# First pair's weight sums on GpSimd, third pair's in the norm's scratch with two accumulating loads; the condition row spread by matmuls, x on one queue

## The chip, the core and the metric

The kernel runs on one core of one Trainium2 chip. The metric is the device time of one execution in microseconds; of a kernel, the median over its runs. In the text, PE is TensorE, DVE is VectorE, ACT is ScalarE, POOL is GpSimd and SP is SyncE, whose queue issues most of the loads. Each engine works through its own instructions in order, so an instruction that waits holds everything that stands behind it on that engine.

## What is computed

A decoder trunk of two layers on a sequence of 512 tokens, model width 1024. Each layer is a half-step SwiGLU feed-forward (FFN), a token mixer (a short gated convolution in layer 0, native sparse attention in layer 1), and a second half-step FFN: six sub-layers, s = 0 to 5, with FFNs at s = 0, 2, 3 and 5. Each sub-layer starts with an RMS norm whose scale and shift, and ends with a gate, that come from a conditioning vector c:

```python
cond = jax.nn.silu(c)
for i in range(DEPTH):
    mod = (cond @ ada_w[i] + ada_b[i]).reshape(bsz, 3, 3, D_MODEL)
    shift, scl, gate = mod[:, :, 0], mod[:, :, 1], mod[:, :, 2]
    h = adaln(x, norm_g[i, 0], shift[:, 0], scl[:, 0])
    x = x + HALF * gate[:, 0, None, :] * swiglu(h, ffn_w_in[i, 0], ffn_w_out[i, 0])
    ...
def swiglu(h, w_in, w_out):
    g, u = jnp.split(h @ w_in, 2, axis=-1)
    return (jax.nn.silu(g) * u) @ w_out
```

All data are float32.

## The kernel before

**Layout.** x lies transposed in SBUF, eight tiles x[0] to x[7] of 128 partitions (128 model columns) by 512 tokens. A float32 product is made of three fast matmuls: each operand is split into a rounded part and the rest (`split`, L168: ACT copies to the rounded type, L169; DVE subtracts, L170), and `mm3` (L172 to L175) adds hi·hi, hi·lo and lo·hi. So each weight tile costs a load (tag `wraw`, three buffers, issued by SP), one ACT pass (`whi`) and one DVE pass (`wlo`).

**The start.** SP loads x[0] to x[5], then the condition c as a load that repeats its row over all 128 partitions (L97, 512 KB), then the first tiles of ada_w (`adaraw`, 512 KB each); GpSimd's queue loads x[6], x[7] and two small tables. `Norm.start` squares the x tiles on ACT (L271), adds them on DVE into `nacc` (L273), sums over partitions on PE (`pr`, L275), and takes the reciprocal root on DVE (`rsqrt`, L201 to L209). ACT applies SiLU to c (L112). DVE multiplies each `adaraw` tile with `cond` and sums (L124): 144 of these give all shifts, scales and gates.

**The FFNs at s = 2, 3 and 5** (function `ffn`, weights f = 1, 2, 3) have 22 hidden tiles. For the first three (j = 0, 1, 2) gate and up are plain products: in `head_start` (matmuls named `hs`) for the first half of the tokens and then for the second half, then `pair`. Each half has its own norm: `Norm.finish` runs a reciprocal root on DVE under high priority and then makes diagonal tiles `dg` (L262) that PE spreads (L263, `pr`); `Norm.piece` (L312 to L315) makes h from them. The later 19 tiles (j = 3 to 21) use `seven_products`: a Strassen-like scheme in which gate and up together take seven half-size products instead of eight. It needs sums of weight quarters. In words, for each j, which the text calls a pair (gate and up):

- `qa`, two quarters wide: SP loads quarters 11 of gate and 22 of up into its halves (L490, L491), and one load on GpSimd's queue adds quarter 21 of gate to both halves (L493, an accumulating load);
- `raw` (L495), the whole gate tile, and `a22`, one quarter of up (L496);
- `qb`, two adds: `qa`'s second half plus raw's first half (L497), and that plus raw's second half (L498), both on DVE;
- then the splits of raw, qa, a22 and qb (ACT `whi`, `qah`, `qbh`; DVE `wlo`, `qal`, `qbl`), the seven products of 12 matmuls each (PE, named `gu`), of which ACT copies the first away at once (`p1`, L520), since its PSUM columns are used again, and the sums of the products on DVE (`e`, L526 to L532).

"First pair" is j = 3, "second" j = 4, "third" j = 5. Where `qa` lies is set by a list (L553 to L555): pool `swa` has two buffers called `own`; the first three pairs use `own`, so the third has to wait until the first pair's `qa` has been split. The pairs behind them turn through two freed pieces of the norm's output (tags `hhi1`, `hlo1`) and `own`. The norm's squares use a scratch of two tiles of 128x512 (`sq`), which is idle from the end of the norm until the next sub-layer's squares.

Hidden tiles are grouped in `FOUR` (6, 6, 6, 4); after each of the first three groups eight output products `y` follow (L567 to L570). The order of the instructions on each engine comes from a scheduler, which places each by priority and by its dependences; the order below is what it made.

Of the kernel before, what the change touches and what calls it, by code (L numbers as in the profile page):

```python
# [13 lines left out]
F32 = mybir.dt.float32  # L14
F32R = mybir.dt.float32r
I32 = mybir.dt.int32
AF = mybir.ActivationFunctionType
ALU = mybir.AluOpType
# [4 lines left out]
P = 128  # L23
D = 1024
T = 512
HT = T // 2
KD = D // P
# [26 lines left out]
def decoder_kernel(ctx, tc, xT, cT, ng, adaw, adab, ffi, ffo, cwi, cw, cwo,  # L54
                   nwi, nwg, pos, w1, w2, qg, kg, nwo, rb, onehot, rowok, out):
    nc = tc.nc

    def pool(es, name, bufs, **kw):
        kw.setdefault("reuse_waits", "tile")
        return es.enter_context(tc.tile_pool(name=name, bufs=bufs, **kw))  # L60
# [7 lines left out]
    wp = pool(ctx, "wp", 4)  # L68
# [8 lines left out]
    def psum(name, tag="mm"):  # L77
        tag = next(six) if tag == "mm" else {"pr": "o"}.get(tag, tag)
        return ps.tile([P, T], F32, name=name, tag=tag, bufs=2)
# [4 lines left out]
    def tmp(name, n=T, tag="t"):  # L84
        bufs, size = TAGS[tag]
        return tp.tile([P, n], F32, name=name, tag=tag, padded_shape=[P, size], bufs=bufs)
# [3 lines left out]
    ap = ada_es.enter_context(tc.tile_pool(name="ada", bufs=4))  # L90
    cond = ap.tile([P, D], F32, name="cond", bufs=1)
    x = [cst.tile([P, T], F32, name=f"x{d}") for d in range(KD)]
    ngs = cst.tile([P, NSUB * KD], F32, name="ngs")
    adabs = cst.tile([P, NSUB * NMOD], F32, name="adabs")
    for d in range(KD):
        (nc.sync if d < KD - 2 else nc.gpsimd).dma_start(x[d], xT[d])
    nc.sync.dma_start(cond, bass.AP(tensor=cT.tensor, offset=cT.offset, ap=[[0, P], [1, D]]))  # L97
    nc.gpsimd.dma_start(ngs, ng)
    nc.gpsimd.dma_start(adabs, adab)
    rowm = cst.tile([P, 1], F32, name="rowm")  # L100
# [4 lines left out]
    ones = cst.tile([P, P], F32, name="ones")  # L105
# [3 lines left out]
    kgs = cst.tile([P, 3], F32, name="kgs")  # L109
    mods = cst.tile([P, NSUB * NMOD], F32, name="mods")  # L110

    nc.scalar.activation(cond, cond, AF.Silu)  # L112

    def mod(s, kind, d):
        c = s * NMOD + kind * KD + d
# [52 lines left out]
    def split(src, hi, lo):  # L168
        nc.scalar.activation(hi, src, AF.Copy)  # L169
        nc.vector.tensor_tensor(lo, src, hi, ALU.subtract)  # L170

    def mm3(o, sh, sl, mh, ml, first, last):  # L172
        nc.tensor.matmul(o, sh, mh, start=first, stop=False)  # L173
        nc.tensor.matmul(o, sh, ml, start=False, stop=False)  # L174
        nc.tensor.matmul(o, sl, mh, start=False, stop=last)  # L175
# [219 lines left out]
    class Hidden:  # L395
# [4 lines left out]
        def keep(self, af):  # L400
            hi = self.fa.tile([P, T], F32R, name="ahi", tag="a")
            lo = self.fa.tile([P, T], F32R, name="alo", tag="a")
            split(af, hi, lo)
            self.hi.append(hi)
            self.lo.append(lo)
# [63 lines left out]
    def ffn(s, f, nrm, nxt, w0, ahead):  # L469
        with ExitStack() as es:  # L470
# [3 lines left out]
            nj = 2  # L474
# [3 lines left out]
            def seven_products(j):  # L478
                QT = KD * P // 2
                quart = lambda c, k: ffi[f, j, c].rearrange("p k n -> p (k n)")[:, k * QT:(k + 1) * QT]  # L480
                raw = wp.tile([P, 2, QT], F32, name="wraw", tag="wraw", bufs=3)
                whi = wp.tile([P, 2, QT], F32R, name="whi", tag="whi", bufs=3)
                wlo = wp.tile([P, 2, QT], F32R, name="wlo", tag="wlo", bufs=3)
                qa = next(sums)()
                a22 = tmp("a22")
                qb = swa.tile([P, 2, QT], F32, name="qb")
                ah_, al_ = (sw.tile([P, 2, QT], F32R, name=f"qa{e}", bufs=2) for e in "hl")
                bh_, bl_ = (sw.tile([P, 3, QT], F32R, name=f"qb{e}") for e in "hl")
                e = sw.tile([P, 4, HT], F32, name="e")
                nc.sync.dma_start(qa[:, 0], quart(0, 0))  # L490
                nc.sync.dma_start(qa[:, 1], quart(1, 1))  # L491
                a21 = quart(1, 0)
                nc.gpsimd.dma_start(qa, bass.AP(tensor=a21.tensor, offset=a21.offset, ap=[a21.ap[0], [0, 2], a21.ap[1]]),  # L493
                                    accum_op=ALU.add)
                nc.sync.dma_start(raw.rearrange("p a b -> p (a b)"), ffi[f, j, 0].rearrange("p k n -> p (k n)"))  # L495
                nc.sync.dma_start(a22, quart(1, 1))  # L496
                nc.vector.tensor_tensor(qb[:, 0], qa[:, 1], raw[:, 0], ALU.add)  # L497
                nc.vector.tensor_tensor(qb[:, 1], qb[:, 0], raw[:, 1], ALU.add)  # L498
                split(raw, whi, wlo)
                split(qa, ah_, al_)  # L500
                split(a22, bh_[:, 0], bl_[:, 0])
                split(qb, bh_[:, 1:3], bl_[:, 1:3])

                def product(o, w, b):
                    for i in range(KD // 2):
                        c = slice(i * P, (i + 1) * P)
                        mh, ml = b(i)
                        mm3(o, w[0][:, c], w[1][:, c], mh, ml, i == 0, i == KD // 2 - 1)

                a11, a12 = [(whi[:, i], wlo[:, i]) for i in range(2)]  # L510
                s3, s1 = [(ah_[:, i], al_[:, i]) for i in range(2)]
                a22, s2, s4 = [(bh_[:, i], bl_[:, i]) for i in range(3)]
                t1, t2, t3, t4 = nrm.blocks
                lo, hi = slice(0, HT), slice(HT, T)
                ox, oy, oz = psum("gu"), psum("gu"), psum("gu")
                both = lambda o: o.rearrange("p (a b) -> p a b", a=2)
                product(oy[:, lo], a11, nrm.quarter(0, 0))
                p1 = tmp("p1", HT, "xr")
                with tc.high_priority():
                    nc.scalar.activation(p1, oy[:, lo], AF.Copy)  # L520
                product(ox[:, lo], a12, nrm.quarter(1, 0))
                product(oy[:, hi], s3, t3)
                product(oy[:, lo], s1, t1)
                product(oz[:, hi], a22, t4)
                product(ox[:, hi], s2, t2)
                nc.vector.tensor_tensor(e[:, 0:2], both(ox), p1[:, None].to_broadcast([P, 2, HT]), ALU.add)  # L526
                nc.vector.tensor_tensor(e[:, 2], oy[:, hi], e[:, 1], ALU.add)
                nc.vector.tensor_tensor(e[:, 1:4:2], oy[:, None, lo].to_broadcast([P, 2, HT]), e[:, 1:3], ALU.add)
                product(oz[:, lo], s4, nrm.quarter(1, 1))
                nc.vector.tensor_tensor(e[:, 1:3], both(oz), e[:, 1:3], ALU.add)  # L530
                nc.scalar.activation(e[:, 0:2], e[:, 0:2], AF.Silu)
                nc.vector.scalar_tensor_tensor(e[:, 0:2], e[:, 0:2], -1.0, e[:, 2:4], op0=ALU.mult, op1=ALU.mult)  # L532
                keep(e[:, 0:2].rearrange("p a b -> p (a b)"))
# [4 lines left out]
            with ExitStack() as tf_es:  # L538
                nrm.alloc_seven(hp, pool(tf_es, "tf", 1))
                h = nrm.hi, nrm.lo  # L540
                with ExitStack() as hw_es:
# [8 lines left out]
            nj += 1  # L550
            sw_es = es.enter_context(ExitStack())

            own, quarter = (partial(swa.tile, [P, 2, KD * P // 2], F32, name="qa", bufs=2),  # L553
                            [partial(hp.tile, [P, 2, KD * P // 2], F32, name="qa", tag=t) for t in ("hhi1", "hlo1")])
            sums = chain((own, own, own), cycle((*quarter, own, own)))  # L555
            sw = pool(sw_es, "sw", 1)
            shift(sw, 64)
            for j in range(nj):
# [1 line left out]
            for p, (j0, j1) in enumerate(FOUR):  # L560
                for j in range(max(j0, nj), j1):
                    seven_products(j)
                n = j1 - j0
                a = (hid.hi[j0:j1], hid.lo[j0:j1])
                if p < len(FOUR) - 1:
                    for d in range(KD):
                        w = ffn_out(f, d, 1, j0, j1)  # L567
                        o = psum("y")
                        project(o, w, 0, a, [(k, k) for k in range(n)], True, True)
                        nc.vector.scalar_tensor_tensor(x[d], o, mod(s, 2, d), x[d], op0=ALU.mult, op1=ALU.add)  # L570
# [4 lines left out]
            for i, d in enumerate(range(0, KD, 2)):  # L575
                if i < 2:
                    ws.append(ffn_out(f, d, 2, j0, j1))
                else:
                    t = (2, 0)[i - 2]
                    to = [tt.tile([P, KD // 2, HT], F32R, name=f"t{e}{t}").rearrange("p a b -> p (a b)") for e in "hl"]  # L580
                    raw = swa.tile([P, 2, KD * P // 2], F32, name="qa", bufs=2).rearrange("p a b -> p (a b)")
# [18 lines left out]
            for d, t in [(d, 0) for d in range(6, KD)] + [(d, HT) for d in range(KD)]:  # L600
                o = psum("ty")
# [631 lines left out]
    ada_es.close()  # L1233
    nrm, nxt = nxt, Norm(3)
    w = ffn(2, 1, nrm, nxt, w, ffn_ahead(2))
    nrm, nxt = nxt, Norm(4)
    w = ffn(3, 2, nrm, nxt, w, lambda: nsa_in(4))
    nrm, nxt = nxt, Norm(5)
    w = nsa(4, nrm, nxt, w, ffn_ahead(3))
    ffn(5, 3, nxt, None, w, None)  # L1240


# [73 lines left out]
```

## Time and profile before

| | us |
|---|---|
| three runs | 1999.37, 2007.13, 2008.69 |
| median | 2007.13 |
| the profiled execution | 2008.19 |
| its span, first to last instruction | 2006.4 |
| PE busy in it | 1932.2 (96%) |
| DVE, ACT, POOL busy | 1493.1, 874.8, 203.1 |

The profile is of one execution. Busy PE is the time in which matmuls were in flight; PE at half its clock is as busy as at full clock, so the granted clock has to be read beside it. "Idle before" an instruction is the time its engine stood still ahead of it, with the instruction or load that ended the wait. "DMA share" is the mean busy share of the 16 DMA engines. Times in the text are counted from the start of the span. The stages in it: FFN s = 0 to 367, convolution to about 570, the FFNs from about 575, 920 and 1640, attention from about 1280.

### The profile page before, as it was taken

The numbers are of one execution on the slowest core, as the hardware profiler recorded it, in microseconds if no ns is written. First come the engines' busy times: TensorE is split into PE (matmuls) and PEld (weight loads), VectorE is DVE, ScalarE is ACT, GpSimd is POOL, SyncE is SP. The second block draws the span as 40 slices with busy tenths as digits, with TensorE's granted clock in tenths as the row PEclk, the third lists the DMA queues.
The fourth block names the chain that finished last, engine by engine and source line by source line (L and its number), as shares of the span: only waits on it lengthen the run. The fifth ranks groups of instructions, "written<-read, shape, count | busy, mean of one in ns | idle before, by whom it ended". The sixth has DMA issues, their size and how long they took to land.

```text
span 2006.4 us, 32443 instructions
## 1 busy us (share of the span) xinstructions
PE 1932.2 (96%) x12644; PEld 1747.7 (87%) x12644; DVE 1493.1 (74%) x2597; ACT 874.8 (44%) x1410; POOL 203.1 (10%) x279
## 2 busy tenths in 40 slices
PE   5999999999988999999999999999999899999999
PEld 3878888798888898999989899999888689898989
DVE  7878888674457686868868686886787978786866
ACT  3322222232225353434535343455777866343532
POOL 0000000100010000000000000001434430000000
PEclk9999999999998999999999999999999999999999
DMA  8888988432235664634566453243211223665622
GB/s 308 304 315 311 328 316 325 156 105 84 84 105 146 165 167 126 163 101 116 157 169 169 131 160 102 68 137 107 54 48 28 84 63 100 181 175 154 170 69 74
DMA packets 113047, 307.40 MB, mean 153 GB/s; under 512 B 13883, under 2 KB 14155, under 8 KB 112892
## 3 DMA queue, kind: packets, MB, share of 16 engines
q1 hardware_dynamic: 97164, 274.81, 40.4%
q0 software_dynamic: 15728, 30.51, 8.9%
q8 instruction: 99, 1.62, 0.3%
q14 instruction: 56, 0.46, 0.1%
HBM read 302.12 MB, written 3.15 MB: 152 GB/s over the span
## 4 chain that ended last, share of the span: by engine, by line
PE 69%; DVE 14%; DMA 9%; ACT 4%; issue 3%; SPq 1%; POOL 0%; DVEq 0%; ACTq 0%; POOLq 0%
PE gu L173 10%; PE gu L174 10%; PE gu L175 10%; DMA adaraw<-in_adaw 7%; PE y L173 6%; PE y L175 6%; PE y L174 6%; DVE wlo L170 3%; DVE adaraw L124 3%; PE cv L174 2%; PE cv L173 2%; PE cv L175 2%; PE hs L173 1%; PE hs L174 1%; PE hs L175 1%
## 5 line engine op out<-in xcount | busy, mean ns | idle before, releaser
L169 ACT ACTIVATE whi<-wraw 128x1024 fp32r<-128x1024 f32 (+2 forms) x283 | 281.8, 999 | 499.8 <-PE y L174 264.5
L170 DVE TENSOR_TENSOR wlo<-wraw,whi 128x1024 fp32r<-128x1024 f32 (+2 forms) x283 | 326.4, 1155 | 59.9 <-ACT whi L169 57.8
L174 PE MATMUL gu<-hlo,whi 128*128 128x256 f32 (+1 forms) x808 | 258.5, 320 | 0.0
L173 PE MATMUL gu<-hhi,whi 128*128 128x256 f32 (+1 forms) x808 | 258.2, 320 | 0.0
L175 PE MATMUL gu<-hhi,wlo 128*128 128x256 f32 (+1 forms) x808 | 257.6, 319 | 0.0
L173 PE MATMUL y<-ahi,whi 128*128 128x512 f32 x587 | 230.2, 395 | 2.9 <-ACT ahi L169 2.9
L174 PE MATMUL y<-alo,whi 128*128 128x512 f32 x587 | 228.7, 392 | 0.8 <-DVE alo L170 0.8
L175 PE MATMUL y<-ahi,wlo 128*128 128x512 f32 x587 | 229.0, 393 | 0.0
L124 DVE CUSTOM_DVE_ANT_0 adaraw<-adaraw,cond 128x1024 f32<-128x1024 f32 x144 | 174.8, 1223 | 37.1 <-DMA adaraw<-in_adaw 34.8
L173 PEld LDWEIGHTS gu<-hhi,whi 128*128 128x128 f32 x808 | 151.7, 188 | 13.0
L175 PEld LDWEIGHTS gu<-hhi,wlo 128*128 128x128 f32 x808 | 151.6, 188 | 12.3
L174 PEld LDWEIGHTS gu<-hlo,whi 128*128 128x128 f32 x808 | 151.7, 188 | 12.0
L493 POOL DMA_DIRECT2D qa<-in_ffi x57 | 68.6, 1204 | 816.8 <-DVE wlo L170 228.4
L173 PE MATMUL gu<-th,qah 128*128 128x256 f32 x456 | 128.9, 283 | 9.6 <-ACT p L520 9.6
L173 PEld LDWEIGHTS y<-ahi,whi 128*128 128x128 f32 x587 | 109.8, 188 | 30.6 <-ACT ahi L169 7.4
L174 PEld LDWEIGHTS y<-alo,whi 128*128 128x128 f32 x587 | 110.6, 188 | 26.9 <-DVE alo L170 3.2
L175 PEld LDWEIGHTS y<-ahi,wlo 128*128 128x128 f32 x587 | 110.6, 188 | 23.8
L570 DVE SCALAR_TENSOR_TENSOR x<-y,mods,x 128x512 f32<-128x512 f32 x72 | 54.0, 750 | 101.2 <-PE y L175 100.4
L173 PE MATMUL gu<-th,qbh 128*128 128x256 f32 x456 | 126.4, 277 | 2.3 <-ACT qbh L169 2.2
L174 PE MATMUL gu<-tl,qah 128*128 128x256 f32 x456 | 128.3, 281 | 0.0
L175 PE MATMUL gu<-th,qal 128*128 128x256 f32 x456 | 128.2, 281 | 0.0
L175 PE MATMUL gu<-th,qbl 128*128 128x256 f32 x456 | 126.2, 277 | 0.2 <-DVE qbl L170 0.2
(303 smaller groups left out, 5205.6 us busy)
## 6 DMA issues: line engine op xcount, KB each, us to landing
adaraw<-in_adaw SPq DMA_DIRECT2D x144, 512.0 KB, 6.0
wraw<-in_ffi SPq DMA_DIRECT2D x119, 512.0 KB, 3.8
qa<-in_ffi SPq DMA_DIRECT2D x114, 256.0 KB, 3.8
qa<-in_ffi POOLq DMA_DIRECT2D x57, 512.0 KB, 6.6
wraw<-in_ffo SPq DMA_DIRECT2D x72, 384.0 KB, 4.0
a<-in_ffi SPq DMA_DIRECT2D x57, 256.0 KB, 4.3
wraw<-in_cwi SPq DMA_DIRECT2D x24, 512.0 KB, 3.3
wraw<-in_nwi SPq DMA_DIRECT2D x20, 512.0 KB, 3.4
```

The source lines that it names most:

```text
L124: nc.vector.tensor_tensor_reduce(out=raw, in0=raw, in1=cond, scale=1.0, scalar=0.0, op0=ALU.mult, op1=ALU.add, accum_out=m)
L169: nc.scalar.activation(hi, src, AF.Copy)
L170: nc.vector.tensor_tensor(lo, src, hi, ALU.subtract)
L173: nc.tensor.matmul(o, sh, mh, start=first, stop=False)
L174: nc.tensor.matmul(o, sh, ml, start=False, stop=False)
L175: nc.tensor.matmul(o, sl, mh, start=False, stop=last)
L493: nc.gpsimd.dma_start(qa, bass.AP(tensor=a21.tensor, offset=a21.offset, ap=[a21.ap[0], [0, 2], a21.ap[1]]), accum_op=ALU.add)
L570: nc.vector.scalar_tensor_tensor(x[d], o, mod(s, 2, d), x[d], op0=ALU.mult, op1=ALU.add)
```

## The change

1. **Condition row.** GpSimd's queue loads c once, as one row (4 KB) into partition 0 of a `wraw` buffer; two matmuls with a row of ones spread it over the partitions into PSUM, and ACT applies SiLU from there in two halves. The load of 512 KB goes. All eight x tiles are on SP's queue.
2. **First pair.** Its two sums `qb` run on GpSimd instead of DVE.
3. **Third pair.** Its `qa` is two tiles of the norm's scratch `sq` instead of an `own` buffer. As these are two tiles, there are two accumulating loads of one half each, and its split is done in two halves.

```diff
+    crow = wp.tile([P, D], F32, name="wraw", tag="wraw", bufs=3)[0:1]
+    nc.gpsimd.dma_start(crow, cT)
     for d in range(KD):
-        (nc.sync if d < KD - 2 else nc.gpsimd).dma_start(x[d], xT[d])
-    nc.sync.dma_start(cond, bass.AP(tensor=cT.tensor, offset=cT.offset, ap=[[0, P], [1, D]]))
+        nc.sync.dma_start(x[d], xT[d])
...
-    nc.scalar.activation(cond, cond, AF.Silu)
+    for c in range(D // T):
+        o = psum("cb", "nat")
+        nc.tensor.matmul(o, ones[0:1], crow[:, c * T:(c + 1) * T], start=True, stop=True)
+        nc.scalar.activation(cond[:, c * T:(c + 1) * T], o, AF.Silu)
...
+                halves = qa if isinstance(qa, list) else [qa[:, 0], qa[:, 1]]
+                nc.sync.dma_start(halves[0], quart(0, 0))
+                nc.sync.dma_start(halves[1], quart(1, 1))
...
+                if qa is halves:
+                    for q in qa:
+                        nc.gpsimd.dma_start(q, a21, accum_op=ALU.add)
+                else:
+                    nc.gpsimd.dma_start(qa, ..., accum_op=ALU.add)
...
-                nc.vector.tensor_tensor(qb[:, 0], qa[:, 1], raw[:, 0], ALU.add)
-                nc.vector.tensor_tensor(qb[:, 1], qb[:, 0], raw[:, 1], ALU.add)
+                eng = nc.gpsimd if j == nj else nc.vector
+                eng.tensor_tensor(qb[:, 0], halves[1], raw[:, 0], ALU.add)
+                eng.tensor_tensor(qb[:, 1], qb[:, 0], raw[:, 1], ALU.add)
...
-            sums = chain((own, own, own), cycle((*quarter, own, own)))
+            sums = chain((own, own, lambda: [tmp("qa", tag="sq") for _ in range(2)]), cycle((*quarter, own, own)))
```

The changed kernel's lines have other numbers: the loads into `qa` are L496 and L497 there, the accumulating loads L501 (halves) and L503, the sums L509 and L510.

**DVE, FFN s = 2, in the second half's reciprocal root.** Before: `rs_` rows are the root, `qb` the first pair's sums, `dg` the diagonal tiles that PE waits for.

```order
L209 SCALAR_TENSOR_TENSOR rs_r_4625<-rs_b,rs_r_4619 128x2
L207 SCALAR_TENSOR_TENSOR rs_a<-rs_r_4625 128x2
L497 TENSOR_TENSOR qb<-qa,wraw 128x512
L208 TENSOR_TENSOR rs_b<-rs_a,nv 128x2
L498 TENSOR_TENSOR qb<-qb,wraw 128x512
L209 SCALAR_TENSOR_TENSOR rs_r_4631<-rs_b,rs_r_4625 128x2
L262 TENSOR_SCALAR dg<-ident,rs_r_4631 128x128 x2
```

Now, on the same engine at the same place:

```order
L214 SCALAR_TENSOR_TENSOR rs_r_4631<-rs_b,rs_r_4625 128x2
L212 SCALAR_TENSOR_TENSOR rs_a<-rs_r_4631 128x2
L213 TENSOR_TENSOR rs_b<-rs_a,nv 128x2
L214 SCALAR_TENSOR_TENSOR rs_r_4637<-rs_b,rs_r_4631 128x2
L267 TENSOR_SCALAR dg<-ident,rs_r_4637 128x128 x2
```

The two sums have left DVE's queue, and the root runs through.

**GpSimd, the FFNs at s = 2 and s = 3.** Before, from the convolution's squares (`nacc`) to attention there is one row, the accumulating loads:

```order
L238 TENSOR_TENSOR nacc<-nacc,sq 128x512 x8
L493 DMA qa<-in_ffi 128x2x512 x38
```

Now (the first `qa` row is the first and second pair's; rows of 128x512 are the third pair's halves; `qb` are the first pair's sums):

```order
L243 TENSOR_TENSOR nacc<-nacc,sq 128x512 x8
L503 DMA qa<-in_ffi 128x2x512 x2
L501 DMA qa<-in_ffi 128x512
L509 TENSOR_TENSOR qb<-qa,wraw 128x512
L501 DMA qa<-in_ffi 128x512
L510 TENSOR_TENSOR qb<-qb,wraw 128x512
L503 DMA qa<-in_ffi 128x2x512 x18
L509 TENSOR_TENSOR qb<-qa,wraw 128x512
L510 TENSOR_TENSOR qb<-qb,wraw 128x512
L501 DMA qa<-in_ffi 128x512 x2
L503 DMA qa<-in_ffi 128x2x512 x16
```

At s = 2 the first sum stands behind the third pair's first accumulating load, at s = 3 ahead of both; all later accumulating loads stand behind the sums.

**SP, FFN s = 2.** Before: `qa_5090`, `qa_5215` and `qa_5340` are the first, second and third pair's, `qa_5673` and `qa_5798` the fourth's and fifth's.

```order
L491 DMA qa_5215<-in_ffi 128x512
L495 DMA wraw_5212<-in_ffi 128x1024
L495 DMA wraw_5337<-in_ffi 128x1024
L184 DMA wraw_5464<-in_ffo 128x768
L490 DMA qa_5798<-in_ffi 128x512
L490 DMA qa_5673<-in_ffi 128x512
L490 DMA qa_5340<-in_ffi 128x512
L496 DMA a22_5091<-in_ffi 128x512
L496 DMA a22_5216<-in_ffi 128x512
L491 DMA qa_5340<-in_ffi 128x512
```

Now (`qa_5346` and `qa_5347` are the third pair's halves, `qa_5683` and `qa_5808` the fourth's and fifth's):

```order
L497 DMA qa_5221<-in_ffi 128x512
L496 DMA qa_5346<-in_ffi 128x512
L497 DMA qa_5347<-in_ffi 128x512
L505 DMA wraw_5218<-in_ffi 128x1024
L505 DMA wraw_5343<-in_ffi 128x1024
L189 DMA wraw_5474<-in_ffo 128x768
L496 DMA qa_5808<-in_ffi 128x512
L496 DMA qa_5683<-in_ffi 128x512
L497 DMA qa_5683<-in_ffi 128x512
L497 DMA qa_5808<-in_ffi 128x512
L506 DMA a22_5097<-in_ffi 128x512
```

The third pair's loads have moved ahead of the second's and third's `raw`, straight behind the second pair's `qa`; the first `a22` stands behind four loads of the fourth and fifth pair, where it stood behind three. At s = 3 the third's loads stand ahead of the second pair's `raw`, and at s = 5 too.

More of the change, by code (lines that the diff above doesn't have):

```diff
@@ L489, in seven_products @@
                 e = sw.tile([P, 4, HT], F32, name="e")
-                nc.sync.dma_start(qa[:, 0], quart(0, 0))
-                nc.sync.dma_start(qa[:, 1], quart(1, 1))
+                halves = qa if isinstance(qa, list) else [qa[:, 0], qa[:, 1]]
+                nc.sync.dma_start(halves[0], quart(0, 0))
+                nc.sync.dma_start(halves[1], quart(1, 1))
                 a21 = quart(1, 0)
-                nc.gpsimd.dma_start(qa, bass.AP(tensor=a21.tensor, offset=a21.offset, ap=[a21.ap[0], [0, 2], a21.ap[1]]),
-                                    accum_op=ALU.add)
+                if qa is halves:
+                    for q in qa:
+                        nc.gpsimd.dma_start(q, a21, accum_op=ALU.add)
+                else:
+                    nc.gpsimd.dma_start(qa, bass.AP(tensor=a21.tensor, offset=a21.offset, ap=[a21.ap[0], [0, 2], a21.ap[1]]),
+                                        accum_op=ALU.add)
                 nc.sync.dma_start(raw.rearrange("p a b -> p (a b)"), ffi[f, j, 0].rearrange("p k n -> p (k n)"))
                 nc.sync.dma_start(a22, quart(1, 1))
-                nc.vector.tensor_tensor(qb[:, 0], qa[:, 1], raw[:, 0], ALU.add)
-                nc.vector.tensor_tensor(qb[:, 1], qb[:, 0], raw[:, 1], ALU.add)
+                eng = nc.gpsimd if j == nj else nc.vector
+                eng.tensor_tensor(qb[:, 0], halves[1], raw[:, 0], ALU.add)
+                eng.tensor_tensor(qb[:, 1], qb[:, 0], raw[:, 1], ALU.add)
                 split(raw, whi, wlo)
-                split(qa, ah_, al_)
+                if qa is halves:
+                    for n, q in enumerate(qa):
+                        split(q, ah_[:, n], al_[:, n])
+                else:
+                    split(qa, ah_, al_)
                 split(a22, bh_[:, 0], bl_[:, 0])
```

## Prediction

> **What bounds the kernel now.** I read the page's busy times first, then the stretches by stage, then PE's waits in the stretches where PE is not full, then the engines that PE waits for.
>
> ```profile
> PE 1932.2 (96%) x12644; PEld 1747.7 (87%) x12644; DVE 1493.1 (74%) x2597; ACT 874.8 (44%) x1410; POOL 203.1 (10%) x279
> ```
>
> The table by stretches (columns: length; busy time and instructions of PE, PEld, DVE, ACT, POOL; granted clock; DMA share; GB/s):
>
> ```profile
> 46.00:125.00 79.00, 79.00 (x348) 65.10 (x347) 66.74 (x103) 26.75 (x35) 0.00 (x0) 1.00 0.85 306
> 590.00:650.00 60.00, 48.83 (x378) 47.85 (x378) 40.74 (x65) 28.48 (x42) 5.88 (x6) 0.89 0.56 142
> 650.00:925.00 275.00, 274.73 (x1965) 255.57 (x1965) 201.63 (x263) 113.66 (x148) 19.20 (x16) 1.00 0.53 145
> 925.00:1000.00 75.00, 69.90 (x574) 68.60 (x573) 63.03 (x130) 42.53 (x71) 4.81 (x4) 0.98 0.49 130
> 1640.00:1720.00 80.00, 75.38 (x623) 73.94 (x623) 65.72 (x133) 42.47 (x70) 7.22 (x6) 0.98 0.54 139
> ```
>
> PE is the bound: in long stretches it is busy without a gap, so what is won ahead of such a stretch goes through to the end. It loses time at the entry of each of the three FFNs at s = 2, 3, 5: 11.2, 5.1 and 4.6 us of gaps in rows two, four and five, and a lower clock on top. PE's waits in those entries, one answer each:
>
> ```profile
> PE pr L263 <- DVE dg L262: 5.9, 1, 5.9
> PE gu L173 <- ACT p L520: 5.0, 1, 5.0
> ```
> ```profile
> PE gu L173 <- ACT p L520: 1.9, 1, 1.9
> PE gu L173 <- ACT qbh L169: 1.6, 1, 1.6
> PE hs L173 <- ACT hhi L314: 1.3, 1, 1.3
> ```
> ```profile
> PE gu L173 <- ACT p L520: 2.7, 1, 2.7
> PE hs L173 <- ACT hhi L314: 1.2, 1, 1.2
> ```
>
> And what the clock did behind them (PE only: length, busy, clock, DMA share):
>
> ```profile
> 600.00:606.20 6.20, 6.15 (x27) 0.51 0.00 0
> 627.00:641.00 14.00, 13.67 (x119) 1.00 0.91 262
> 646.40:650.60 4.20, 4.20 (x20) 0.52 0.89 203
> 995.30:998.80 3.50, 3.50 (x19) 0.53 0.94 206
> 1708.70:1712.10 3.40, 3.15 (x15) 0.51 0.85 285
> ```
>
> Each larger wait is followed by 3.4 to 6.2 us at half clock, so that about half of that time is lost as well: 3.0, 2.0, 1.6 and 1.5 us (busy time by the clock that is missing).
>
> **The change part by part.** *A, the first pair's sums, s = 2.* DVE's timeline:
>
> ```profile
> 592.05 0.16 DVE L207 SCALAR_TENSOR_TENSOR rs_a<-rs_r 128x2 f32<-128x2 f32 x1
> 597.99 0.69 DVE L497 TENSOR_TENSOR qb<-qa,wraw 128x512 f32<-128x512 f32 x1 [5.78 <-DMA qa<-in_ffi]
> 598.72 0.69 DVE L498 TENSOR_TENSOR qb<-qb,wraw 128x512 f32<-128x512 f32 x1
> 599.51 0.29 DVE L262 TENSOR_SCALAR dg<-ident,rs_r 128x128 f32<-128x128 f32 x1
> ```
>
> The sum waits 5.78 us for the accumulating load, and the last two steps of the reciprocal root stand behind it. A step follows on the one before after 0.2 us (estimated from their 0.16 us), so without the two sums `dg` starts three steps after 592.05, at 592.65: 6.9 us earlier. PE, which waited 5.9 us, then never stops there, and the 3.0 us of half clock behind it go too: 8.9 us at most. At least it is the 6.9 by which DVE moves, since from `dg` on DVE and ACT also have a long run of work for the second half and PE's regained clock does not shorten it. I take 7.9.
>
> The sums cost GpSimd two adds of 128x512:
>
> ```profile
> L493 POOL DMA_DIRECT2D qa<-in_ffi x57 | 68.6, 1204 | 816.8 <-DVE wlo L170 228.4
> L238 POOL TENSOR_TENSOR nacc<-nacc,sq 128x512 f32<-128x512 f32 x8 | 13.4, 1674 | 552.4 <-ACT sq L236 552.4
> 626.45 1.05 ACT L169 ACTIVATE qbh<-qb 128x1024 fp32r<-128x1024 f32 x1
> ```
>
> 1.67 us each against DVE's 0.69. The first pair's load lands by 597.99; with two adds and an accumulating load issued between them (1.2 us of GpSimd at most) the second sum is done by about 603. ACT reads `qb` at 626.45, or 7.9 earlier now: 15 us of cover. At s = 3 and 5 the cover is longer, as the sums there never waited. The Trainium skill, GPSIMD Engine Reference, section 3 (Performance versus the Vector engine), speaks against this edit: an elementwise add of two inputs belongs on VectorE, since GpSimd measured 1.96 times its time. The row here says 2.4 times; by the page's ratio the two adds would take 2.7 us instead of 3.3, and under that cover the sum is the same unless the two engines hinder each other (a rival below).
>
> At s = 5 the two sums stand in the same root without a wait:
>
> ```profile
> 1663.87 0.68 DVE L497 TENSOR_TENSOR qb<-qa,wraw 128x512 f32<-128x512 f32 x1
> 1664.59 0.69 DVE L498 TENSOR_TENSOR qb<-qb,wraw 128x512 f32<-128x512 f32 x1
> ```
>
> They go from DVE's path to the `hhi` for which PE waits 1.2 us, and are worth about that, 1.2 us. At s = 3 the order of before has one of the two ahead of the root and one behind it, so half counts: 0.6 of PE's 1.3 us.
>
> *B, C, D, the third pair's scratch, s = 2, 3, 5.* The chain of waits at s = 2, in order of time, and what ACT did:
>
> ```profile
> 626.58 1.24 DVE qal L170
> 627.83 0.33 SPq L490
> ...
> 630.10 13.27 DMA qa<-in_ffi x2
> ```
> ```profile
> 643.52 1.06 ACT L169 ACTIVATE qah<-qa 128x1024 fp32r<-128x1024 f32 x1 [9.78 <-DMA qa<-in_ffi]
> 645.95 0.36 ACT L520 ACTIVATE p<-gu 128x256 f32<-128x256 f32 x1
> 991.85 1.06 ACT L169 ACTIVATE qah<-qa 128x1024 fp32r<-128x1024 f32 x1 [6.70 <-DMA wraw<-in_ffo]
> 1706.11 1.06 ACT L169 ACTIVATE qah<-qa 128x1024 fp32r<-128x1024 f32 x1 [7.28 <-DMA wraw<-in_ffo]
> ```
>
> The third pair's buffer comes free with the first pair's `qal`; then come two loads and the accumulating one, in a stretch with a DMA share of 0.91 (627 to 641). ACT, in order, waits 9.78 us for it, and the second pair's `p1` stands behind. At s = 3 and 5 it is the same instruction with 6.70 and 7.28 us (the load named there belongs to another tile; by the chain at s = 2 I read it as the accumulating load). With the scratch, idle since the norm's last square, the loads can go before 606, where the DMA engines stand idle (share 0.00). So PE's waits for `p` go, with the half clock behind each: B 5.0 + 2.0 = 7.0; C 1.9 + 1.6, and the 0.6 above, 4.1; D 2.7 + 1.5, and the 1.2, 5.4. The split in halves is one more instruction on ACT and on DVE, a fraction of the 1.06 us that the whole takes, where they waited for 7 to 10.
>
> Late next is the first `a22`. At s = 2 it now stands behind four loads instead of three, and PE can wait about 1 us for it; at s = 3, where PE waits 1.6 us for its split, nothing ahead of it waits for the first pair's `qal` any more, and it may come up to 1 us earlier. I put both at zero, with 1.5 us to each side.
>
> The Trainium skill, TensorE: Matmul & The Clock Gate, part 1, has the clock halved only after an idle window of about 3.4 us. Here 1.9 and 2.7 us of waiting for `p` were enough. By the page's rule the half clock at s = 3 and 5 would have another cause and stay, and the sum would be 3.1 us smaller; the rows decide, as nothing else stood still there.
>
> *E, the start.*
>
> ```profile
> 2.59 7.01 DMA x<-in_xT
> 13.48 1.88 PE pr L275 x8
> 125.72 1.93 PE pt L676 x4
> ```
> ```profile
> 10.00:20.00 10.00, 1.86 (x8) 1.78 (x8) 7.23 (x25) 4.21 (x6) 0.00 (x0) 1.00 0.95 366
> ```
> ```profile
> L124 DVE CUSTOM_DVE_ANT_0 adaraw<-adaraw,cond 128x1024 f32<-128x1024 f32 x144 | 174.8, 1223 | 37.1 <-DMA adaraw<-in_adaw 34.8
> ```
> ```profile
> ngs<-in_ng POOLq DMA_DIRECT2D x1, 24.0 KB, 5.8
> ```
>
> The last x tile lands at 9.6, and the DMA engines are full. 508 KB fewer are 1.4 us at 366 GB/s. By the new order DVE multiplies the first `adaraw` while PE sums the squares: the 1.22 us that one takes move into the 1.88 us in which DVE had no squares left to add, 1.1 us more. E = 2.5; up to 3.4 if the x tiles come closer together on one queue. SP issues two x loads more and one load less, GpSimd the reverse. The price of the new way: two matmuls of 128x512 took 1.93 us at 125.72, at half clock 3.9; if the row, issued within the first 2 us, lands as slowly as the small table (5.8 us), both halves are spread by 11.7, and the last square behind them in ACT's queue still makes the 13.48 at which PE begins to sum. So E is nothing at worst, or half a us below. The `wraw` buffer that the row takes is free by then as well, and the third weight load, the first to need it, stands behind four `adaraw` loads that wait for DVE. From 46 on PE is full, so E goes through.
>
> Sum: 7.9 + 7.0 + 4.1 + 5.4 + 2.5 = 26.9 us. Against the profiled execution, 2008.19 (span 2006.4 and 1.8 around it), that is 1981.3; this execution is 1.1 us above the median of the runs. I say 1981.
>
> **The rivals.** *The burst remains.* The DMA share of 0.85 to 0.94 behind each wait says that the loads are the bound there, and the fourth pair's load takes the third's place ahead of `p1`. Against: the third pair's loads leave that burst for an idle stretch, and the fourth's split stands one product later in ACT's queue. Only A, the DVE parts at s = 3 and 5 and E remain, 12.2 us: 1996. *The shared port.* The same page of the Trainium skill (section 1, Specifications) has GpSimd share its SBUF ports with VectorE, with contention where a DVE instruction reads two SBUF inputs. If DVE stood still for GpSimd's two adds, 3.3 us in each FFN where it feeds PE, 10 us of the gain go: 1991. No run here shows it yet. *GpSimd's queue, the slower side.* At s = 2 and 5 the first sum stands behind the third pair's accumulating load, which waits for the scratch and SP. If that comes later than ACT's read of `qb`, ACT's queue stands with `p1` in it. From 15 us of lateness on each us is lost; at 25 us, B, C and D are not won and each entry loses 10 us and 1.6 of clock: 2008 - 12 + 35 = 2031. Against: the scratch is free before SP gets there. *It does nothing.* The scratch is handed over only when the old wait ends and the root meets another wait: 2007.
>
> **How the numbers follow.** Forecast 0.74, burst 0.12, port 0.06, nothing 0.05, GpSimd's queue 0.03. With the low ends of the terms (A 6.9, no clock back at B, C and D, E at -0.5, `a22` against) the forecast reaches to 1990, with the high ends to 1977; the runs of before spread over 9 us, so 4 us below that is possible: 1973. The burst takes the range up to 1996. Half a per cent, 10 us, is about what a measurement of this kernel can tell from no change: faster 0.92, same 0.05, slower 0.03.
>
> **What would show it.** Right: no DVE wait ahead of `dg` at s = 2, no PE wait there and full clock behind; ACT's third `qah` without a wait at all three entries; `p` gone from PE's waits. Wrong: a PE wait for `p` or `qbh` of over 3 us, DVE instructions longer beside GpSimd's sums, or the first sums of `adaraw` starting no earlier than before.

## The result, and the profile after

The changed kernel takes 1987.19 us (median of 5 runs, 1979.69 to 1991.76) against 2007.13 us (median of 5 runs, 1999.37 to 2012.35): a ratio of 0.9912, 95% interval 0.9887 to 0.9938, so the change is faster. That is 19.9 us by the medians, where the prediction's sum was 26.9. The profiled execution is the slowest of the five, 1991.76 us (span 1990.0), and is 16.4 us of span shorter than the one before.

PE's busy time in the page, and the waits of PE at the three entries, one answer for s = 2, s = 3 and s = 5 each (total, times, longest):

```profile
PE 1935.0 (97%) x12648; PEld 1747.0 (88%) x12648; DVE 1497.1 (75%) x2594; ACT 876.3 (44%) x1414; POOL 211.1 (11%) x287
```
```profile
PE gu L180 <- DVE qbl L175: 1.8, 1, 1.8
PE gu L178 <- ACT p L536: 0.6, 1, 0.6
```
```profile
PE gu L178 <- ACT qbh L174: 1.9, 1, 1.9
PE hs L179 <- DVE hlo L320: 1.0, 1, 1.0
PE hs L178 <- ACT hhi L319: 0.9, 1, 0.9
```
```profile
PE pr L268 <- DVE dg L267: 3.7, 1, 3.7
PE hs L178 <- ACT hhi L319: 1.2, 1, 1.2
PE gu L178 <- ACT qbh L174: 0.7, 1, 0.7
```

At s = 2 the waits of 5.9 and 5.0 us are down to nothing and 0.6, as forecast; 1.8 us for `qbl` are new. At s = 5 a wait for `dg` has come that was not there before, 3.7 us. The granted clock behind the waits (length, PE busy, clock, DMA share, GB/s):

```profile
600.00:660.00 60.00, 57.61 (x440) 1.00 0.61 167
926.30:933.10 6.80, 6.80 (x32) 0.50 0.65 116
970.70:974.10 3.40, 3.40 (x19) 0.50 1.07 239
1653.40:1656.80 3.40, 3.40 (x18) 0.51 0.00 1
```

The half clock is gone at s = 2, and so are the stretches at 995 and 1708 of before; new ones have come at s = 3 (926, 971) and s = 5 (1653). The third pair's first split on ACT, whose waits of 9.78, 6.70 and 7.28 us the change was to end, has now no wait at any entry:

```profile
621.18 1.15 ACT L174 ACTIVATE qah<-qa 128x512 fp32r<-128x512 f32 x2
970.19 1.14 ACT L174 ACTIVATE qah<-qa 128x512 fp32r<-128x512 f32 x2
1687.06 1.14 ACT L174 ACTIVATE qah<-qa 128x512 fp32r<-128x512 f32 x2
```

Where did the rest go? DVE's timeline at s = 5, in the second half's root, and GpSimd's and SP's in the same stretch:

```profile
1644.67 0.16 DVE L213 TENSOR_TENSOR rs_b<-rs_a,nv 128x2 f32<-128x2 f32 x1
1644.74 2.31 DVE L320 SCALAR_TENSOR_TENSOR hlo<-hfull,mods,hhi 128x256 fp32r<-128x256 f32 x1
1646.98 1.95 DVE L214 SCALAR_TENSOR_TENSOR rs_r<-rs_b,rs_j 128x2 f32<-128x2 f32 x1
1648.85 0.47 DVE L320 SCALAR_TENSOR_TENSOR hlo<-hfull,mods,hhi 128x256 fp32r<-128x256 f32 x1
...
1651.42 0.48 DVE L267 TENSOR_SCALAR dg<-ident,rs_r 128x128 f32<-128x128 f32 x2
```
```profile
1644.55 0.90 POOL L501 DMA_DIRECT2D qa<-in_ffi  x1 [11.54 <-DVE rs_a L212]
1645.14 1.62 POOL L509 TENSOR_TENSOR qb<-qa,wraw 128x512 f32<-128x512 f32 x1
1646.64 0.96 POOL L501 DMA_DIRECT2D qa<-in_ffi  x1
1647.25 1.65 POOL L510 TENSOR_TENSOR qb<-qb,wraw 128x512 f32<-128x512 f32 x1
```
```profile
1641.38 0.33 SPq L496 DMA_DIRECT2D qa<-in_ffi  x1
1642.10 0.33 SPq L497 DMA_DIRECT2D qa<-in_ffi  x1
```

The `hlo` beside GpSimd's adds at s = 2 (three in one row) and at s = 3:

```profile
593.79 3.49 DVE L320 SCALAR_TENSOR_TENSOR hlo<-hfull,mods,hhi 128x256 fp32r<-128x256 f32 x3
924.86 1.28 DVE L320 SCALAR_TENSOR_TENSOR hlo<-hfull,mods,hhi 128x256 fp32r<-128x256 f32 x1
```

An `hlo` of 128x256 that takes 0.48 us elsewhere takes 2.31, and a step of the root on 128x2 that takes 0.15 takes 1.95: 1.83 + 1.80 = 3.63 us, while GpSimd adds from 1645.14 to 1648.90. That is the size of PE's wait of 3.7. A busy engine can thus be a waiting one: the lost time lies in the length of the instruction, and no wait shows it. At s = 2 three `hlo` beside the two adds take 3.49 us (1.27 without), at s = 3 one takes 1.28 (0.48). The rows of GpSimd and SP tell why the adds fall into the root at s = 5: the first sum stands in GpSimd's queue behind the third pair's accumulating load, which waits for loads that SP issues from 1641.38 on, when the norm's last squares have left the scratch. (The row names `rs_a` as what ended that wait; I read it as the first of these loads, since loads into `qa` took 2.6 us and more to land in this stretch.)

### The profile page after: what moved, and what is told of

Same layout as the page of the kernel before. It is cut to its first block, busy times and chain, and to the rows that moved or that the text cites. A ratio compares the mean times of both kernels' runs of the same rounds, so it can differ in the third digit from the quotient of the medians.

```text
span 1990.0 us, 32476 instructions
## 1 busy us (share of the span) xinstructions
PE 1935.0 (97%) x12648; PEld 1747.0 (88%) x12648; DVE 1497.1 (75%) x2594; ACT 876.3 (44%) x1414; POOL 211.1 (11%) x287
## 4 chain that ended last, share of the span: by engine, by line
PE 75%; DVE 12%; DMA 7%; ACT 3%; issue 2%; SPq 0%; POOL 0%; DVEq 0%; ACTq 0%; POOLq 0%
PE gu L178 10%; PE gu L180 10%; PE gu L179 10%; PE y L178 6%; PE y L179 6%; PE y L180 6%; DMA adaraw<-in_adaw 6%; DVE wlo L175 3%; PE hs L178 2%; PE hs L179 2%; DVE adaraw L129 2%; PE hs L180 2%; PE cv L179 2%; PE cv L178 2%; PE cv L180 2%
## 5 line engine op out<-in xcount | busy, mean ns | idle before, releaser
L503 POOL DMA_DIRECT2D qa<-in_ffi x54 | 64.9, 1202 | 756.5 <-DMA qa<-in_ffi 289.1
L179 PE MATMUL gu<-tl,qbh 128*128 128x256 f32 x456 | 126.7, 278 | 0.0
```

## The experiments

To see which entry wins what, I take from each profiled trace its lead over the kernel before ahead of a stage and behind it; the difference, in us, is what the stage won. The places: at the start the `pr` behind `dg` (20.45 in before); at s = 2 from the second half's first `pr` (587.39) to the fourth `p` (699.84); at s = 3 from the nineteenth to the twenty-second `p` (910.22, 1004.85); at s = 5 from the second half's first `pr` (1659.24) to the 41st `p` (1719.11).

| kernel | start | s = 2 | s = 3 | s = 5 | median, us | ratio to before (95%) |
|---|---|---|---|---|---|---|
| changed kernel | 2.9 | 13.8 | -1.5 | -0.7 | 1987.2 | 0.9912 (0.9887-0.9938) |
| only_start | 2.5 | 0.5 | -0.2 | -3.1 | 2001.4 | 0.9979 (0.9959-0.9999) |
| only_scratch | -0.7 | 7.4 | 4.8 | 3.7 | 1990.0 | 0.9916 (0.9895-0.9937) |
| only_gpsimd | -0.6 | 12.0 | 1.2 | -2.5 | 1996.4 | 0.9960 (0.9940-0.9979) |
| sums_on_dve | 3.3 | 6.7 | 4.0 | 3.7 | 1984.0 | 0.9914 (0.9894-0.9935) |
| gpsimd_s2 | 3.3 | 13.3 | 2.8 | 4.5 | 1980.6 | 0.9888 (0.9867-0.9909) |
| gpsimd_extra | 2.4 | 13.4 | 2.5 | -0.4 | 1984.4 (one run) | |
| sums_first | 3.3 | 13.6 | 3.7 | 2.7 | 1985.0 | 0.9901 (0.9885-0.9918) |
| late_sums | 2.5 | 14.9 | 3.2 | 3.0 | 2003.2 | 0.9990 (0.9973-1.0006) |
| late_sums_slot | 3.3 | 16.0 | 3.7 | 4.2 | 1972.9 | 0.9839 (0.9817-0.9862) |
| late_s2 | 2.6 | 16.4 | 2.7 | 3.6 | 1974.0 | 0.9849 (0.9823-0.9874) |
| small_tile | 2.6 | 13.7 | 0.7 | -2.3 | 2011.6 | 1.0033 (1.0016-1.0050) |
| wide_tile | 3.0 | 12.5 | -0.2 | -1.6 | 2011.1 (one run) | |

How far one such number can be trusted is seen where the code is as before: -0.7 and -0.6 at the start (only_scratch, only_gpsimd), but -3.1 at s = 5 in only_start, where PE waited 4.6 us for `p` instead of 2.7 and a stretch at half clock was 6.8 us long instead of 3.4:

```profile
PE gu L178 <- ACT p L536: 4.6, 1, 4.6
```

**sums_on_dve**, the first pair's sums back on DVE, the other parts kept:

```diff
-                eng = nc.gpsimd if j == nj else nc.vector
+                eng = nc.vector
```

> The changed kernel with the first pair's two sums back on VectorE at s = 2, 3 and 5; scratch and start stay. Theory, standstill: in the changed kernel VectorE stands still while GpSimd adds (hlo 2.31 and rs_r 1.95 us at s = 5 instead of 0.48 and 0.15), and this ate what s = 3 and s = 5 should have won. Then PE's 3.7 us wait for dg at s = 5 goes, the entries of s = 3 and s = 5 win 3.5 and 4.2 us over before instead of losing 1.5 and 0.7, and at s = 2 the 5.9 us wait for dg comes back with its half clock (7.9): 1987.2 - 9.9 + 7.9 = 1985. Rival, the loads: the third pair's loads, moved ahead into the root, hold VectorE up whoever adds, so s = 3 and s = 5 stay as they are and only s = 2 gets worse: 1995.

Measured 1984.0. PE's waits at s = 2 and at s = 5:

```profile
PE pr L268 <- DVE dg L267: 7.1, 1, 7.1
PE gu L180 <- DVE qbl L175: 0.2, 1, 0.2
```
```profile
PE gu L178 <- ACT qbh L174: 1.3, 1, 1.3
PE hs L178 <- ACT hhi L319: 1.2, 1, 1.2
PE pr L260 <- DVE nacc L243: 0.3, 1, 0.3
```

The wait for `dg` moves from s = 5 to s = 2, the entries at s = 3 and 5 win 4.0 and 3.7. The theory of the loads falls: at s = 5, with the same early loads and no GpSimd add, nothing stands still. As a whole the new place of the sums bought nothing here: 1984.0 without it, 1987.2 with it, and the intervals overlap.

**gpsimd_s2**, GpSimd adds at s = 2 alone:

```diff
+                eng = nc.gpsimd if j == nj and s == 2 else nc.vector
```

> The changed kernel with the first pair's sums on GpSimd at s = 2 alone, on VectorE at s = 3 and s = 5. Standstill: the wait for dg at s = 5 (3.7 us) and the long hlo and rs_r go, s = 3 keeps its clock at 926 to 933, s = 2 stays as it is: 1987.2 - 9.9 = 1977. The loads: dg at s = 5 is as late as now, and VectorE has two sums more on its way there: 1987 to 1989.

Measured 1980.6, two thirds of the way. s = 5 wins 4.5 and its wait for `dg` is down to 0.2 us. s = 3 wins 2.8, no more than the other traces with GpSimd's sums there (2.5 and 3.7), so the -1.5 of the changed kernel's trace at s = 3 isn't the standstill's alone; the expectation had put half of its gain there.

**gpsimd_extra**, an unused GpSimd instruction more in each later pair, an add at s = 2, a copy at s = 3, a memset at s = 5:

```diff
+                if j > nj + 2:
+                    extra = tmp("extra", tag="sq")
+                    if s == 2:
+                        nc.gpsimd.tensor_tensor(extra, raw[:, 0], raw[:, 1], ALU.add)
+                    elif s == 3:
+                        nc.gpsimd.tensor_copy(extra, raw[:, 0])
+                    else:
+                        nc.gpsimd.memset(extra, 0.0)
```

> The changed kernel with one more GpSimd instruction of 128x512 in each later pair, whose result is not used: an add of two tiles at s = 2, a copy of one tile at s = 3, a memset at s = 5. Standstill by SBUF inputs: VectorE's instructions that read two tiles of SBUF (the sums of qb, 0.69 us, and the subtractions of the splits, 1.22 us) get longer by the time they share with an add, up to 1.3 to 1.6 us more; those that read PSUM (e from gu) stay at their time; the memset lengthens nothing, and the copy is open. If the standstill is not made by GpSimd's adds, no VectorE instruction gets longer beside them.

DVE and GpSimd (POOL) in one timeline at s = 2, start and length of each, and the same with the copy at s = 3:

```profile
663.64 0.95 DVE L175 TENSOR_TENSOR wlo<-wraw,whi 128x768 fp32r<-128x768 f32 x1
663.93 1.81 POOL L514 TENSOR_TENSOR extra<-wraw 128x512 f32<-128x512 f32 x1 [27.41 <-DMA wraw<-in_ffi]
664.51 1.78 DVE L509 TENSOR_TENSOR qb<-qa,wraw 128x512 f32<-128x512 f32 x1
666.32 0.69 DVE L510 TENSOR_TENSOR qb<-qb,wraw 128x512 f32<-128x512 f32 x1
...
668.32 2.20 POOL L514 TENSOR_TENSOR extra<-wraw 128x512 f32<-128x512 f32 x1 [2.58 <-DMA wraw<-in_ffi]
669.29 0.75 DVE L595 SCALAR_TENSOR_TENSOR x<-y,mods,x 128x512 f32<-128x512 f32 x1
669.95 1.39 DVE L175 TENSOR_TENSOR wlo<-wraw,whi 128x768 fp32r<-128x768 f32 x1
671.26 1.20 POOL L503 DMA_DIRECT2D qa<-in_ffi  x1 [0.73 <-DMA qa<-in_ffi]
671.27 0.68 DVE L509 TENSOR_TENSOR qb<-qa,wraw 128x512 f32<-128x512 f32 x1
```
```profile
1009.77 1.16 POOL L516 COPY extra<-wraw 128x512 f32<-128x512 f32 x1 [25.91 <-DMA wraw<-in_ffi]
1010.37 1.10 DVE L509 TENSOR_TENSOR qb<-qa,wraw 128x512 f32<-128x512 f32 x1
```

The add comes while DVE subtracts two tiles and has to wait for it; then DVE's `qb` (0.69 us elsewhere) waits for the add. `x<-y`, which reads PSUM and one tile of SBUF, keeps its 0.75 us beside the second add, and the subtraction behind it takes 1.39 instead of 0.95. Beside a copy `qb` takes 1.10; beside the memsets at s = 5 and beside the issue of an accumulating load (671.26) all keep their times. So in these rows one of the two waits until the other's instruction is done, and only where both read SBUF and DVE reads two tiles of it. The Trainium skill, SBUF — State Buffer, section "SBUF: two separate sides", has this as a port pair that is locked for a whole instruction, where the loser stands; the trace agrees in each of these rows. Undisturbed, GpSimd's add takes 1.28 us, 1.9 times DVE's 0.69. The Trainium skill, GPSIMD Engine Reference, section 3, measured 1.96 times, which the trace comes near to. The 1.67 us that the prediction took was not that of an undisturbed add.

**late_sums**, the sums on DVE, held back by their data until the second `tl` is written:

```diff
+                if j == nj:
+                    one = sp.tile([P, 1], F32, name="one", bufs=1)
+                    nc.vector.tensor_scalar(one, nrm.tl[0][:, 0, 0:1].bitcast(F32), 0.0, 1.0, op0=ALU.mult, op1=ALU.add)
+                    nc.vector.scalar_tensor_tensor(qb[:, 0], halves[1], one, raw[:, 0], op0=ALU.mult, op1=ALU.add)
```

> The first pair's sums on VectorE at all three entries, but held back by their data until the second tl is written, behind the root and the pieces of the second half; GpSimd adds nothing. Standstill: no VectorE instruction is longer than its kind, the waits for dg are gone at s = 2 and s = 5, and VectorE does 1.4 us of sums at s = 2 in place of 2.2 us of standing still: 1987.2 - 9.9 - 0.8 = 1976. The loads: the entries of s = 3 and s = 5 still give nothing: 1987.

Measured 2003.2, a miss of 27 us. The entries do what was expected (s = 3 wins 3.6 counted from the root's `pr` on, as the next expectation has it), but between them, with no wait of PE, the lead shrinks: from one `p` to the next 9.88 us instead of 9.52. The new one-column tile was the suspect, which three kernels test:

**late_sums_slot**, **late_s2** and **small_tile**:

```diff
+                    one = sp.tile([P, 1], F32, name="one", tag="rs_a", padded_shape=[P, 16], bufs=2)
...
+                if j == nj and s == 2:
...
+    one = sp.tile([P, 1], F32, name="one", bufs=1)
+    nc.vector.memset(one, 1.0)
```

The first line goes into late_sums and makes it late_sums_slot; with the second besides it is late_s2; the last two go into the changed kernel.

> The held-back sums of late_sums once more; the one-column tile that holds them back takes a slot that the root uses, so that no tile of the program lies elsewhere than in the changed kernel. In late_sums the three entries won 14.9, 3.6 and 3.0 us over before (13.8, -1.5 and -0.7 in the changed kernel), but 128x256 matmuls took 280 ns instead of 276 and the long stretches lost some 18 us. Theory, layout: the new tile, not the held-back sums, made the matmuls slower; now 276 ns again and the entries' gain shows: 1987.2 - 1 - 3 - 3.7 = 1979.5. Rival: VectorE's later sums slow PE: 2003 again.

> Held back at s = 2 alone, where VectorE waited for the load in the kernel before; at s = 3 and s = 5 the sums stand in the root on VectorE as they did before. Same slot as in late_sums_slot. Entries as measured in the kernels with these parts: 14.9 at s = 2, 3.5 at s = 3 (2.8 to 4.0), 4.1 at s = 5 (3.7 to 4.5), so 1.2 us under the kernel with GpSimd's sums at s = 2 alone (1980.6): 1979. If standing still at s = 2 cost nothing, it is no faster than that kernel: 1981.

> The changed kernel with one more tile of one column, written once by a memset at the start and used by nothing; all that is allocated behind it moves. Theory, layout: 128x256 matmuls of the pairs take 280 ns instead of 276 and the time rises by some 18 us: 2005. Rival, the tile does nothing: 276 ns and 1987.

Matmuls of the pairs at 690 to 905, in the changed kernel and in small_tile (count, busy, mean ns):

```profile
L178 PE MATMUL gu<-th,qah 128*128 128x256 f32 x120 | 33.1, 276 | 0.0
L178 PE MATMUL gu<-hhi,whi 128*128 128x256 f32 x119 | 32.9, 276 | 0.0
```
```profile
L180 PE MATMUL gu<-th,qah 128*128 128x256 f32 x122 | 34.1, 280 | 0.0
L180 PE MATMUL gu<-hhi,whi 128*128 128x256 f32 x120 | 33.9, 282 | 0.0
```

A tile that nothing uses costs the changed kernel 24 us (2011.6), and the held-back sums without it take 1972.9: the tile slowed PE, not the sums. PE, ACT and GpSimd do the same instructions in the same order in both kernels; DVE has one memset more. 0.36 us in each of the 54 steps from `p` to `p` are 19 of the 24 us; where the others lie wasn't followed up.

late_sums_slot and late_s2 are the fastest kernels of the study, 6.6 and 5.0 us below their expectations; their traces lead by 5.3 and 7.7 us more in the attention, where nothing was changed. At s = 2 they win 16.0 and 16.4, against 13.3 to 13.8 with GpSimd's sums (12.5 in wide_tile), and the only wait of PE left there is 0.2 us (late_sums_slot's row; late_s2 has the same):

```profile
PE gu L180 <- DVE qbl L175: 0.2, 1, 0.2
```

**wide_tile**, the unused tile 16 columns wide:

```diff
-    one = sp.tile([P, 1], F32, name="one", bufs=1)
+    one = sp.tile([P, 16], F32, name="one", bufs=1)
```

> The changed kernel with the unused tile of small_tile made 16 columns (64 bytes in each partition) instead of one. With the one column, a pair took 9.88 us instead of 9.52 and 128x256 matmuls 280 to 282 ns instead of 276. If that hangs on where the operands lie within 64 bytes, all lies as in the changed kernel again, a pair takes 9.52 us and the run about 1987 us. If any displacement costs it, or the tile itself does: 9.88 us and 2011 us.

Measured 2011.1 (one run), 9.89 us from `p` to `p`: so a tile of 64 bytes costs as much as one of 4.

**only_start**, **only_scratch**, **only_gpsimd**: one part of the diff each, in the kernel before.

> The kernel before with the new start alone (row spread by matmuls, x on one queue). As predicted, E = 2.5 us at the start (traces of kernels with the new start: dg 2.4 to 3.3 us earlier): 2004.7 - 2.5 = 2002. Rival, the start is worth the 4.5 us by which the changed kernel led behind the first FFN: 2000.

> The kernel before with the third pair's sums in the norm's scratch alone; the first pair's sums on VectorE. The parts as measured in the kernel with all sums on VectorE: 6.7 at s = 2, 3.5 at s = 3, 4.0 at s = 5: 2004.7 - 14.2 = 1990.5. Rival, the burst remains: none of the three, 2004.7.

> The kernel before with the first pair's sums on GpSimd alone. Standstill: 7 us won at s = 2, some 3 lost at s = 3 and 4.9 at s = 5 (a wait for dg of 3.7 us with its half clock): 2004.7 + 1 = 2006. Without a standstill, as the prediction's term A and its shares at s = 3 and 5 have it (7.9 + 0.6 + 1.2): 1995.

The start measured 2001.4 (4.1 us, interval 0.2 to 8.2, which doesn't tell 2.5 from 4.5), the scratch 1990.0, as expected. GpSimd's sums alone measured 1996.4, near to the figure without a standstill, but not for that reason: they won 12.0 at s = 2, 5 more than expected, and at s = 5, where no wait for `dg` came, they lost 2.5 with a longer wait for `p`:

```profile
PE gu L173 <- ACT p L531: 4.5, 1, 4.5
```
```profile
1638.52 1.28 POOL L504 TENSOR_TENSOR qb<-qa,wraw 128x512 f32<-128x512 f32 x1 [6.13 <-PE ty L174]
1639.88 1.27 POOL L505 TENSOR_TENSOR qb<-qb,wraw 128x512 f32<-128x512 f32 x1
```

Without the scratch's loads ahead of them the sums ran before the root (`pr` at 1642.34), where DVE mostly reads PSUM; one `nacc` took 1.01 us instead of 0.42:

```profile
1640.42 1.01 DVE L238 TENSOR_TENSOR nacc<-nacc,sq 128x256 f32<-128x256 f32 x1
```

That the loss of 2.5 comes from GpSimd is not shown: only_start, with the sums on DVE, waited as long for `p` there and lost 3.1. The wait for `dg` came only with both parts together; the last experiment changes their order in GpSimd's queue.

**sums_first**, the changed kernel with the sums ahead of the third pair's accumulating loads in GpSimd's queue at s = 5:

```diff
+                        if s == 5:
+                            nc.gpsimd.tensor_tensor(q[:, 0:1], q[:, 0:1], zero[0], ALU.add)
                         nc.gpsimd.dma_start(q, a21, accum_op=ALU.add)
...
+                if j == nj and s == 5:
+                    zero[0] = sp.tile([P, 1], F32, name="zero", tag="rs_a", padded_shape=[P, 16], bufs=2)
+                    nc.gpsimd.tensor_scalar(zero[0], qb[:, 1, 0:1], 0.0, None, op0=ALU.mult)
```

> The changed kernel, at s = 5 with the first pair's two sums ahead of the third pair's accumulating loads in GpSimd's queue (a small instruction that adds zero times a number of qb to one column of the scratch holds the loads back). With the new sums but without the scratch GpSimd added at 1638.5 to 1641, ahead of the second half's root, and dg at s = 5 came without a wait; in the changed kernel the sums stand behind the third pair's loads and run at 1645.1 to 1648.9, in the root. Theory, queue and standstill together: the standstill costs much only where it falls into the root, so with the sums at about 1639 again the 3.7 us wait for dg and its half clock go, s = 5 wins some 4 us over before instead of losing 0.7: 1987.2 - 4.9 = 1982. Rival, the standstill alone: it costs the same 3.6 us wherever in the entry GpSimd adds, and s = 5 stays as it is: 1987.

```profile
1635.19 1.28 POOL L511 TENSOR_TENSOR qb<-qa,wraw 128x512 f32<-128x512 f32 x1 [5.46 <-PE ty L179]
1636.54 1.27 POOL L512 TENSOR_TENSOR qb<-qb,wraw 128x512 f32<-128x512 f32 x1
```

The sums run ahead of the root, PE doesn't wait for `dg`, and s = 5 wins 2.7 instead of losing 0.7. The trace settles that the place in the root costs the wait; the medians (1985.0 and 1987.2) alone would not, their intervals overlap.

## Why the prediction was right, and where it was wrong

The forecast of 1981 was 6 us low; the measured time lies inside the stated range. Three of the mechanisms came out (the root that runs through at s = 2, the third pair's early loads, the start), one did not (D). One sign of being wrong that the prediction named came true: DVE instructions longer beside GpSimd's sums. By its steps, in the order of the prediction:

- **A and B, s = 2, 14.9 us:** 13.8; 13.3 to 13.8 in five traces, 12.5 in wide_tile. No wait for `dg`, full clock, `p` down to 0.6 us. But the two don't add: GpSimd's sums alone win 12.0 and the scratch alone 7.4. With `dg` early, the wait for `p` is down to 0.2 us even without the scratch (only_gpsimd); ACT stands 5.69 us for the third `qah` there, where it stood 9.78. What is missing to the 16.0 and 16.4 of the held-back sums is about the 2.2 us by which three `hlo` stood still. PE's wait of 1.8 us for `qbl`, down to 0.2 in those kernels, is where it would show; the way from one to the other is argued, not traced.
- **C, s = 3, 4.1 us:** the waits for `p` are gone as said. -1.5 in this trace, but 2.5 and 3.7 in others with GpSimd's sums there (0.7 and -0.2 in the two with slower matmuls). This trace had 10.2 us at half clock behind waits of 0.9 to 1.9 us, about 5 us lost. How much the term was too large, these traces can't tell: 1 us by the middle of 2.5 and 3.7, more with this one. The first `a22`, put at zero, fits: PE's wait for `qbh` is 1.9 us here (1.6 before) and 0.8 and 0.9 in sums_first and gpsimd_extra.
- **D, s = 5, 5.4 us:** this step failed. -0.7 in this trace, and -0.4, -2.3 and -1.6 in the others with the sums at the same place. The wait for `p` went, but a wait for `dg` of 3.7 us and 3.4 us at half clock took its place. The prediction said that the cover at s = 3 and 5 is longer than at s = 2, and asked only who waits for the sums, not where in the root they run and what DVE does then. Two of its rivals did this together: the sums stood behind the third pair's load in GpSimd's queue, and the shared port made DVE stand for them, 3.6 us at s = 5 where 3.3 were named for each FFN. Each alone did little: without the queue (only_gpsimd, sums_first) the adds ran before the root, without GpSimd (sums_on_dve) the root ran through at s = 5. In sums_on_dve and only_scratch no half clock is left at s = 3 and 5, so that of before did hang on the waits for `p`, as the prediction took it. The 0.06 that the port had was too little; its 1991 lies 4 us from the measured time, the forecast 6.
- **E, the start, 2.5 us:** `dg` 2.9 us earlier, 2.4 to 3.3 in all traces with this start. The first product of `adaraw` begins at 11.54 instead of 15.70, beside PE's sums, as said, for 1.1 us; PE's sum itself begins at 11.68 instead of 13.48, 1.8 us earlier where the bytes were to give 1.4.

The four entries of the profiled trace give 13.8 - 1.5 - 0.7 + 2.9 = 14.5 of its 16.4 us; the other 1.9 lie in stretches where nothing was changed. With 3 for C, the middle of two other traces, it would be 19.0, and the medians say 19.9, but that closeness is partly luck. So, in part, is it that the time lies inside the range: the low end of D was 3.9, and the low ends that the prediction names add up to 1992, not 1990. The price of lost clock was a term that no trace could give as exactly as the prediction had it.

## What to carry to other kernels

A sum moved to GpSimd cost DVE nothing here only where DVE read no two SBUF tiles beside it, so ask where in the program it will run, and what stands ahead of it in GpSimd's queue; a transfer put ahead can push it into the worst place. Where the trouble is that an instruction waits too early in its engine's order, holding it back on the same engine was better here than moving it (at s = 2, with the sums on DVE at s = 3 and 5 in both, 1974.0 against 1980.6; 16.4 us won there against 13.3). And before a slower experiment is explained by its idea, compare the mean time of the matmuls it shares with the other kernel.

## What the runs showed of the hardware

- GpSimd and DVE stand for each other, up to a whole instruction: an add of 1.28 us took 1.81 and 2.20, a `qb` of 0.69 took 1.78. Shown for instructions of DVE with two SBUF tiles against an add or copy of GpSimd; not for PSUM readers, the memset or the issue of a load.
- One more tile of one column, or of 16, makes the 128x256 matmuls take 280 to 282 ns instead of 276 and the kernel 24 us slower. The place in SBUF of what is allocated behind it is the likely reason, but the traces keep no addresses; sums_first and late_sums_slot have more instructions and stay at 9.52 us, so one instruction more is not enough. The rule stays open.
- Half clock comes in stretches of 3.41 us and two or three times that, and in each trace all of them begin on one grid of 3.413 us: in the kernel before at 367.15, 599.26, 643.63, 995.21 and 1708.59, which is 68, 81, 184 and 393 steps behind the first. The grid lies elsewhere in each execution. The Trainium skill, TensorE: Matmul & The Clock Gate, part 1, has a window of about 3.4 us that runs free of the kernel; the grid agrees. At the three entries, in all 14 traces, every step of the grid at full clock in which PE was busy for 40% or less was followed by one at half clock, and none of 70% or more; between these both occurred. This bears on why the same waits don't always bring it: at s = 3 waits of 1.0 and 0.9 us fell into one step in the changed kernel (first row, 44% busy; 6.8 us at half clock followed) and into two in sums_first (68% and 72%; none followed):

```profile
922.88:926.29 3.41, 1.50 (x10) 1.00 0.23 79
```
```profile
923.17:926.58 3.41, 2.33 (x16) 1.00 0.32 116
926.58:929.99 3.41, 2.44 (x21) 1.00 0.29 101
```

- In the attention before s = 5, where nothing was changed, the traces lost and won up to 8 us against each other, so the times of single executions of this kernel can't tell less than that.
